# Seven products for every pair of the second feed-forward, with 56 sums made ahead

## The chip, the core and the metric

The kernel runs on one core of a Trainium2 chip. The core has a matrix engine (TensorE, PE in the profile), VectorE (DVE), ScalarE (ACT), GpSimd (POOL) and SyncE (SP), which run side by side and wait for each other through semaphores. Data lies in DRAM, in SBUF (128 partitions) and, for the results of matmuls, in 8 banks of PSUM. SP and GpSimd issue the transfers of this kernel; 16 DMA engines carry them out. The metric is the time of one execution on the device in microseconds.

## The reference

One layer of a streaming encoder, on 256 tokens of 2048 features in float32: a SwiGLU feed-forward, a block that mixes a linear recurrence and an RG-LRU branch under gates, a cross-attention to 256 memory tokens, a second SwiGLU feed-forward, and a last norm. In short:

```python
x = x + 0.5 * swiglu(rms_norm(x, ffn1_norm), ffn1_w_up, ffn1_w_down)
h = rms_norm(x, mix_norm); proj = h @ w_in
x = x + (sigmoid(gate_a) * (y_a @ w_branch_a) + sigmoid(gate_b) * (y_b @ w_branch_b)) @ w_out
x = x + cross_attention(rms_norm(x, xattn_norm), rms_norm(mem, mem_norm), wq, wkv, wo)
x = x + 0.5 * swiglu(rms_norm(x, ffn2_norm), ffn2_w_up, ffn2_w_down)
return rms_norm(x, final_norm)

def swiglu(h, w_up, w_down):
    gate, up = split(h @ w_up, 2)          # w_up: 2048 x 11264
    return (silu(gate) * up) @ w_down      # w_down: 5632 x 2048
```

All weights are float32 and are read from DRAM once; the matmuls that follow keep nearly float32 precision.

## The kernel before

**Three matmuls for one.** A float32 value is cut into a high and a low part: ACT rounds `raw` into the high part `h`, DVE subtracts to get the low part `l` (helper `split`). A product is then three fast matmuls: high by high, high by low, low by high (helper `three`). Every weight tile of 128 x 2048 (1 MiB) is loaded by SP into a buffer `raw`, split into `h` and `l`, and multiplied; the next weight tiles are asked for two ahead (`weights`, `prepare`).

**The feed-forward.** The up-projection runs over 11 groups `g` of 512 hidden features (512 gate and 512 up columns) and in each over 8 pairs `p`, each of 256 input features. A pair is a product of 2 x 2 blocks: two halves of the tokens and two blocks of 128 features on one side, those blocks and gate or up on the other. There are three ways to do it (`PRODUCTS`, `ffn_order`):

- `plain`: eight products of blocks, 24 matmuls of 512 columns, into four sums in PSUM. Buffers: `raw`, `h`, `l`.
- `fast`: seven products (a Strassen-Winograd scheme), 21 matmuls, into seven sums. It needs four sums of weight blocks (`td`) beside the weights, so a pair takes the buffers `raw`, `td`, `h`, `l` and the two parts of `td` (`h` and `tl`), six in all. On the side of the tokens it needs sums `xs` of the operand's blocks.
- `mixed`: eight products, laid so that they add into the seven sums of a group whose other pairs are fast.

When a group is done, its sums are added up (tile `ev`), go through SiLU and the product, are transposed, split (`hidop`), and wait for the down-projection, whose tiles (`wd`) are laid between the later groups.

**Sums made ahead.** A fast pair's four sums `td` cost DVE four subtractions on its way. For the pairs in the table `MADE` of the second feed-forward they are made earlier, in the middle of the program between the two feed-forwards, where DVE has time. `make_sums` lets GpSimd load the weight tile into a buffer `made`, DVE subtract in place four times, and GpSimd write the tile to DRAM (`kept`). In the second feed-forward SP then loads three quarters of the weight tile into `raw` and the finished sums into `td` (`td<-kept`). `make_ahead` spreads the makes evenly over the weight tiles of the middle.

**Buffers.** All these tiles come from one ring of nine buffers of 8 KiB a partition, `big`. While a feed-forward's own pools are open, four more belong to it; those of the second open only when the last tile of the middle's pools is done with.

**The order.** The code only records operations. A planner (`Flow.arrange`) then plays them through with a price for each (`Flow.price`), hands out buffers, and fixes the order in which each engine's instructions stand. A transfer is priced by its bytes and by a fixed time until it has landed (1.9 us before); a buffer counts as free once the planner believes that its last user is done. On the chip each engine goes through its instructions strictly in that order and waits for semaphores. Since one helper emits everything, all rows of the profile carry one line, L464, and tiles are told apart by name.

Of the kernel before, what the change touches and what calls it, by code (L numbers as in the profile page):

```python
# [14 lines left out]
P = 128  # L15
T = 256
# [4 lines left out]
NG = DFF // 512  # L21
# [9 lines left out]
for _name, _n in [  # L31
# [9 lines left out]


MIXED = {
    "ffn1": {1: (0, 2, 4, 6), 3: (6,)},
    "ffn2": {1: (4, 6), 3: ()},
}
MADE = [(g, p) for g in range(1, NG) for p in range(8) if p not in ((4, 6) if g < 3 else (1, 2, 3, 5, 6))]


def ffn_order(name):  # L50
    mixed = MIXED[name]
    out, down = [("plain", 0, p) for p in range(8)], [("down", 0, 1, c, 0) for c in range(4)]
    for g in range(1, NG):
        if g < 3:
            out += [("mixed" if p in mixed[1] else "fast", g, p) for p in (0, 1, 2, 3, 5, 4, 7, 6)]
        else:
            out += [("mixed" if p in mixed[3] else "fast", g, p) for p in (1, 3, 0, 6, 4, 2, 5, 7)]
        if g > 2 and g % 2:
            down = [("down", g - 2, 2, c, b) for c in range(4) for b in (g - 2, g - 1)]
        n = 2 if g < 3 else 4  # L60
        out, down = out + down[:n], down[n:]
    return out + [("down", NG - 2, 2, c, b) for c in range(4) for b in (NG - 2, NG - 1)]
# [116 lines left out]
LAG = {"PE": 0.24, "DVE": 0.15, "ACT": 0.16, "POOL": 0.16, "SP": 0.1}  # L179
# [4 lines left out]
class Flow:  # L184
# [69 lines left out]
    def price(self, op, method, args, kw, outs):  # L254
        q = op.queue.name
        n = outs[0].cells.size if outs else 0
        if method == "dma_start":
            n = n or args[1].cells.size
            op.moved = n * 512 / 2 ** 20 * (5.2 if "accum_op" in kw else 2.9)
            op.busy = 0.9 if q == "POOL" else 0.06  # L260
        elif method == "transpose":
            op.busy += 0.099
        elif q == "PE":
            op.busy += n / 2400 + 0.0137 if not op.turn else 0.021 if n <= 32 else 0.07 + n * 1.05e-3
        elif q == "DVE":
            n = max(n, kw["in_"].cells.size) if method == "tensor_reduce" else n
            per = {"reciprocal": 6.2, "tensor_tensor_scan": 2.2}.get(method, 1.042)
            op.busy = n * per / 1000 + 0.07
        elif q == "ACT":
            op.busy = n * 0.838e-3 + 0.095 + (0.1 if "accum_out" in kw else 0)  # L270
            op.table = args[2] if args[2] in TABLES else None
        else:
            op.busy = 1.0
# [16 lines left out]
    def arrange(self):  # L290
# [2 lines left out]
        ops = self.ops  # L293
        for op in ops:
            op.after = [a for a in getattr(op, "extra", ())]
            op.spent = op.busy + LAG[op.queue.name] + (op.moved + 1.9 if op.moved else 0)
        for op in ops:
            op.waits = len(op.deps)
            for d in op.deps:
# [20 lines left out]
        dma = reached = 0.0  # L320
# [19 lines left out]
        while events:  # L340
            t, e = heappop(events)
            if free[e] > t + 1e-9:
                continue
            while later[e] and later[e][0][0] <= reached + AHEAD:
                enter(heappop(later[e])[2])
            best, soon = None, 1e18
            for op in cand[e]:
                if best is not None and (not last or best.turn or op.due - STICK > best.due):
                    break
                if best is not None and not op.turn:  # L350
                    continue
                r = op.ready
                if op.moved:
                    r = max(r, dma - BACKLOG)
                if r <= t + 1e-9:
                    for ring in {x.ring for x in op.takes}:
                        fit = ring.fit(op, self)
                        r = max(r, fit[-1][0] if fit else 1e18)
                if r <= t + 1e-9:
                    best = op  # L360
                else:
                    soon = min(soon, r)
            if best is None:
                if soon < 1e17:
                    heappush(events, (soon, e))
                continue
            op = best
            cand[e].remove(op)
            op.start = t
            sequence.append(op)  # L370
            busy = op.busy
            if op.table is not None and op.table != table:
                table = op.table
                busy += 1.3
            if e == "PE":
                busy += 0.1 * (op.turn != last)
                last = op.turn
            free[e] = t + busy
            op.end = t + busy + LAG[e]
            if op.moved:  # L380
                dma = max(dma, t + busy) + op.moved
                op.end = dma + 1.9
            woken = {e}
            if e == "PE" and op.nominal > reached:
                reached = op.nominal
                woken.update(names)
            for ring in {x.ring for x in op.takes}:
                fit = ring.fit(op, self)
                for x in op.takes:
                    if x.ring is ring:  # L390
                        f = fit.pop(0)
                        ring.take(op, f)
                        x.place = f[1]
                        scope = ring.places[f[1]][0].scope
                        if scope is not None:
                            self.opened = max(self.opened, scope)
                            live[scope] += 1
                        if f[2] is not None:
                            for u in f[2].users:
                                if u is not op:  # L400
                                    u.extra.append(op)
                woken.update(names)
            if op.scope is not None:
                live[op.scope] -= 1
            for x in op.tiles:
                x.left -= 1
                x.ends = max(x.ends, op.end)
                if not x.left:
                    x.ring.free.append((x.ends, x.place, x))
                    if x.ring.places[x.place][0].scope is not None:  # L410
                        live[x.ring.places[x.place][0].scope] -= 1
                    woken.update(names)
            for s in op.after:
                kind = s.deps[op]
                if kind is None:
                    r = t
                elif s.queue is op.queue and not op.moved:
                    r = t + busy + (0.1 if kind and e in ("DVE", "ACT") else 0)
                else:
                    r = op.end  # L420
                s.ready = max(s.ready, r)
                s.waits -= 1
                if not s.waits:
# [45 lines left out]
def block_kernel(tc: tile.TileContext, xT, xin, memT, vec, gfin, bgate, lruw, wu1, wd1, win, wv,  # L469
                 wg, wab, wout, wq, wk, wvm, wo, wu2, wd2, out_):  # L470
    flow = Flow(tc)
    pe, dve, act, sp, gps = flow.queues
# [26 lines left out]
    def slot(dt=F32, name="slot"):  # L499
        return slots.tile([P, 1024], dt, name=name, tag="slot")  # L500
# [4 lines left out]
    def bank(name="acc"):  # L505
        return psum.tile([P, 512], F32, name=name, tag="acc")
# [17 lines left out]
    xt = [const.tile([P, 4 * T], F32, name=f"x{q}") for q in range(4)]  # L524
    x = [xt[k // 4][:, (k % 4) * T:(k % 4 + 1) * T] for k in range(KT)]
    ident = col("ident", 0, P)
# [34 lines left out]
    between = len(plan)  # L561
# [16 lines left out]
    between = between + 2, len(plan) - between - 6  # L578
# [22 lines left out]
    sums_kept, makers = {}, []  # L601

    def make_ahead(i):
        n, pieces = len(MADE), between[1]
        if 0 <= i < pieces:
            for j in range(i * n // pieces, (i + 1) * n // pieces):
                makers.append((i + 2, make_sums(*MADE[j])))
        while makers and (makers[0][0] == i or i == pieces):
            makers.pop(0)[1]()
# [222 lines left out]
        act.activation(o, acc[:, :T], ACT.Copy)  # L832
        return o

    def turned(tile, n=2):

        accs = [bank(), bank()]
        for m in range(4):
            for t in range(2):
                pe.transpose(accs[m // 2][:, m % 2 * T + t * P:][:, :P], tile[:, t * 512 + m * P:][:, :P], ident)  # L840
        return accs

    def normed(ops, c, gain):

# [564 lines left out]
    accs = []  # L1409
    for g in range(8):  # L1410
# [4 lines left out]
        if g % 2:  # L1415
            merge(g // 2, accs)
            accs = []
# [7 lines left out]
    for c in range(4):  # L1425
        accs = [bank(), bank()]
# [12 lines left out]
    for m in range(KT):  # L1439
        acc = product(xs3.tiles, weights("q", m), late)  # L1440
# [77 lines left out]

    def to_ffn(c):
        out = []  # L1520
        sums2.append(operand_pairs("ffn2", turned(xt[c]), "ffn2_norm", c, slot(name="xg"), out))
        pairs2.extend(out)
        if c < 2:
            sums2.pop(0)()

    for c in range(4):
# [129 lines left out]
```

## Time and profile before

| | us |
|---|---|
| median of 3 runs | 2453.64 (2452.77 to 2455.08) |
| the profiled execution's own time | 2456.57 |
| its span | 2454.8 |
| PE busy | 2423.6 |
| DVE busy | 2010.7 |
| ACT busy | 1405.8 |
| GpSimd busy | 61.7 |

605 MB move in the span, 247 GB/s on average. The first feed-forward runs until about 690 us, the middle until about 1760, the second feed-forward from there to the end. A row of a group gives the count, then busy time and mean duration (ns), then the idle time of the engine just before such instructions and what ended it. PE's matmuls overlap: one lasts 0.39 us in the records, and the next starts 0.23 us after it.

### The profile page before, as it was taken

How to read it: one execution, taken by the hardware profiler on the slowest of the kernel's cores; microseconds unless marked ns; L12 is line 12 of the kernel's file. 1: busy time of each engine (PE TensorE's matmuls, PEld its weight loads, DVE VectorE, ACT ScalarE, POOL GpSimd, SP SyncE). 2: the span in 40 equal slices, each digit the busy share in tenths (PEclk: the TensorE clock that was granted, in tenths of full speed). 3: DMA queues.
4: the chain of work that ended last, by engine and by line, in shares of the span. 5: the costliest groups of instructions: out<-in, count | busy, mean ns of one | idle time of the engine just before them, and what ended most of it. 6: DMA issues, size and time to landing. Idle time of an engine off the chain costs nothing. (4 is left out here: it accounts for less than half of the span.)

```text
span 2454.8 us, 30751 instructions
## 1 busy us (share of the span) xinstructions
PE 2423.6 (99%) x12166; PEld 2018.0 (82%) x12166; DVE 2010.7 (82%) x2171; ACT 1405.8 (57%) x1408; POOL 61.7 (3%) x102
## 2 busy tenths in 40 slices
PE   9999999999999999999999999999999999999998
PEld 8888888888888887888788788888878788888887
DVE  8999999999855767687676777667769999999995
ACT  8566666666654443576434644545646566666663
POOL 0000000000000000000000000000000000000000
PEclk9999999999999999999999999999999999999999
DMA  8567888778745566767777676666787666666672
GB/s 308 188 228 257 257 260 254 257 251 264 243 152 196 203 243 218 275 242 272 260 269 268 241 292 243 259 227 232 290 321 286 242 244 244 244 244 244 244 287 111
DMA packets 89712, 605.14 MB, mean 247 GB/s; under 512 B 9952, under 2 KB 10208, under 8 KB 21472
## 3 DMA queue, kind: packets, MB, share of 16 engines
q1 hardware_dynamic: 75024, 501.38, 55.5%
q0 software_dynamic: 13824, 100.67, 13.3%
q8 instruction: 95, 1.56, 0.2%
q10 hardware_dynamic: 720, 1.13, 0.1%
q14 instruction: 49, 0.40, 0.0%
HBM read 538.13 MB, written 39.85 MB: 235 GB/s over the span
## 5 line engine op out<-in xcount | busy, mean ns | idle before, releaser
L464 DVE TENSOR_TENSOR l<-raw,h 128x2048 fp32r<-128x2048 f32 (+2 forms) x428 | 875.7, 2051 | 226.3 <-ACT h L464 115.8
L464 ACT ACTIVATE h<-raw 128x2048 fp32r<-128x2048 f32 (+2 forms) x428 | 736.6, 1725 | 536.0 <-PE acc L464 145.1
L464 PE MATMUL acc<-h,xh 128*128 128x512 f32 x1248 | 469.9, 391 | 2.8 <-ACT h L464 2.4
L464 PE MATMUL acc<-h,xl 128*128 128x512 f32 x1248 | 449.9, 389 | 0.0
L464 PE MATMUL acc<-h,hidop 128*128 128x512 f32 x1408 | 442.2, 390 | 0.0
L464 PE MATMUL acc<-h,ops 128*128 128x512 f32 x1664 | 412.5, 392 | 1.2 <-DVE gate L464 1.2
L464 ACT ACTIVATE h<-td 128x1024 fp32r<-128x1024 f32 (+1 forms) x244 | 286.8, 1182 | 208.3 <-DVE td L464 182.8
L464 PE MATMUL acc<-ops,h 128*128 128x512 f32 x1152 | 392.7, 398 | 0.4 <-DVE ops L464 0.4
L464 PEld LDWEIGHTS acc<-h,ops 128*128 128x128 f32 x1664 | 311.1, 188 | 65.5 <-DVE gate L464 1.5
L464 DVE TENSOR_TENSOR tl<-td,h 128x1024 fp32r<-128x1024 f32 (+1 forms) x244 | 333.0, 1373 | 22.1 <-ACT h L464 14.4
L464 PEld LDWEIGHTS acc<-h,hidop 128*128 128x128 f32 x1408 | 262.9, 188 | 53.9 <-ACT ev L464 0.2
L464 PE MATMUL acc<-ops,l 128*128 128x256 f32 x1152 | 273.6, 282 | 8.1 <-DVE l L464 8.1
L464 PEld LDWEIGHTS acc<-h,xh 128*128 128x128 f32 x1248 | 233.5, 188 | 56.1 <-ACT h L464 7.4
L464 PEld LDWEIGHTS acc<-h,xl 128*128 128x128 f32 x1248 | 234.3, 188 | 48.6
L464 PE MATMUL acc<-l,hidop 128*128 128x512 f32 x704 | 265.8, 389 | 0.0
L464 PEld LDWEIGHTS acc<-ops,l 128*128 128x128 f32 x1152 | 213.4, 190 | 29.0 <-DVE l L464 9.0
L464 PEld LDWEIGHTS acc<-ops,h 128*128 128x128 f32 x1152 | 203.2, 189 | 32.1 <-DVE ops L464 0.7
L464 PE MATMUL acc<-l,ops 128*128 128x512 f32 x832 | 221.0, 389 | 0.0
L464 PE MATMUL acc<-l,xh 128*128 128x512 f32 x688 | 198.8, 390 | 0.0
L464 PEld LDWEIGHTS acc<-l,ops 128*128 128x128 f32 x832 | 155.6, 188 | 32.2
L464 PE MATMUL acc<-tl,xh 128*128 128x512 f32 x560 | 174.3, 391 | 0.3 <-DVE tl L464 0.2
L464 PEld LDWEIGHTS acc<-l,hidop 128*128 128x128 f32 x704 | 132.2, 188 | 27.4
(172 smaller groups left out, 1893.2 us busy)
## 6 DMA issues: line engine op xcount, KB each, us to landing
raw<-wu SPq DMA_DIRECT2D x128, 1024.0 KB, 6.8
raw<-wd SPq DMA_DIRECT2D x72, 1024.0 KB, 6.3
raw<-win SPq DMA_DIRECT2D x40, 1024.0 KB, 4.8
made<-wu POOLq DMA_DIRECT2D x36, 1024.0 KB, 5.2
kept<-made POOLq DMA_DIRECT2D x36, 1024.0 KB, 6.2
td<-kept SPq DMA_DIRECT2D x36, 1024.0 KB, 6.6
raw<-wg SPq DMA_DIRECT2D x32, 1024.0 KB, 5.4
raw<-wu SPq DMA_DIRECT2D x36, 768.0 KB, 4.3
```

Of the source, the lines that this page charges most:

```text
L464: getattr(op.queue.real, method)(*map(real, args), **{k: real(v) for k, v in kw.items()})
```

## The change

In the second feed-forward the first group and the four mixed pairs of the second and third group become fast pairs (`MIXED`), so that all 88 pairs take seven products. `MADE` grows from 36 pairs to 56: all 24 of the first three groups, and four instead of three of the eight in each later group (pair 2 is added to 0, 4 and 7). The makes are spread over 16 weight tiles fewer, so they end earlier. In the planner, transfers that GpSimd issues are reckoned to land later: 3.2 us with an accumulation, 4.6 for a load into SBUF, 5.8 for a write to DRAM, and 1.9 as before for all others. For the first group's operand sums, the third quarter's are now made before the feed-forward begins, and the last quarter of x is transposed in halves, so that one bank is taken at a time.

```diff
 MIXED = {
-    "ffn1": {1: (0, 2, 4, 6), 3: (6,)},
-    "ffn2": {1: (4, 6), 3: ()},
+    "ffn1": {0: "plain", 1: (0, 2, 4, 6), 3: (6,)},
+    "ffn2": {0: "fast", 1: (), 3: ()},
 }
-MADE = [(g, p) for g in range(1, NG) for p in range(8) if p not in ((4, 6) if g < 3 else (1, 2, 3, 5, 6))]
+MADE = [(g, p) for g in range(NG) for p in range(8) if p in ((0, 2, 4, 7) if g > 2 else range(8))]
...
-    out, down = [("plain", 0, p) for p in range(8)], [("down", 0, 1, c, 0) for c in range(4)]
+    out, down = [(mixed[0], 0, p) for p in range(8)], [("down", 0, 1, c, 0) for c in range(4)]
...
+            op.lands = 1.9 if q != "POOL" else 3.2 if "accum_op" in kw else 4.6 if op.tiles - {args[0].tile} == set() else 5.8
...
-            op.spent = op.busy + LAG[op.queue.name] + (op.moved + 1.9 if op.moved else 0)
+            op.spent = op.busy + LAG[op.queue.name] + (op.moved + op.lands if op.moved else 0)
...
-                op.end = dma + 1.9
+                op.end = dma + op.lands
...
-        n, pieces = len(MADE), between[1]
+        n, pieces = len(MADE), between[1] - 16
...
-        sums2.append(operand_pairs("ffn2", turned(xt[c]), "ffn2_norm", c, slot(name="xg"), out))
+        halves = turned(xt[c]) if c < 3 else (turned_half(xt[c], y) for y in range(2))
+        sums2.append(operand_pairs("ffn2", halves, "ffn2_norm", c, slot(name="xg"), out))
         pairs2.extend(out)
-        if c < 2:
+        if c < 3:
             sums2.pop(0)()
```

Two places where the order of instructions moves. In the rows, the numbers of the buffers are kept; they rise in the order in which the planner lays the tiles down.

The first place is on DVE in the middle of the program, while the first half's recurrence ends: the last of the four subtractions in a buffer `made`, and the split that is the next to use that buffer, which has to wait for GpSimd's write (a semaphore `DMASW`). Before:

```order
L464 TENSOR_TENSOR made_7274<-made_7274 128x512 [waits DVE_49]
L464 TENSOR_TENSOR ya_7283<-acc_7220,ostd_7332 128x256 [waits DVE_49]
L464 RECIPROCAL ostd_7332<-ostd_7332 128x256
L464 SCALAR_TENSOR_TENSOR ya_7283<-ya_7283,vt_74,silu_5987 128x256 [waits DVE_49]
L464 TENSOR_TENSOR ya_7283<-acc_7221,ostd_7332 128x256 [waits DVE_49]
L464 TENSOR_TENSOR plain_7337<-plain_7337,rstd_5469 128x256
L464 SCALAR_TENSOR_TENSOR ya_7283<-ya_7283,vt_74,silu_5987 128x256 [waits DVE_49]
L464 TENSOR_TENSOR plain_7337<-acc_7285,lo_7399 128x256 [waits Activation_49]
L464 TENSOR_TENSOR plain_7337<-plain_7337,rstd_5469 128x256 [waits DVE_49]
L464 TENSOR_TENSOR l_7414<-raw_7217,h_7270 128x2048 [waits DMAHW1_49,DMASW7_49]
```

The same stretch of the program in the changed kernel:

```order
L465 TENSOR_TENSOR made_7124<-made_7124 128x512 [waits DVE_49] x3
L465 TENSOR_TENSOR l_7221<-raw_7084,h_7139 128x2048 [waits DMAHW6_49,DMASW7_49]
L465 TENSOR_TENSOR plain_7129<-acc_7131,lo_7243 128x256 [waits PE_49,Activation_49]
L465 TENSOR_TENSOR l_7254<-raw_7181,h_7235 128x2048 [waits DMAHW7_49,PE_49]
L465 RECIPROCAL ostd_7248<-ostd_7248 128x256 [waits Activation_49]
L465 TENSOR_TENSOR plain_7129<-plain_7129,rstd_5469 128x256 [waits DVE_49]
L465 TENSOR_TENSOR ya_7289<-acc_7170,ostd_7248 128x256 [waits DVE_49]
L465 RECIPROCAL ostd_7248<-ostd_7248 128x256
L465 TENSOR_TENSOR l_7309<-raw_7191,h_7275 128x2048 [waits DMAHW0_49,DMASW3_49,Activation_49]
```

Between the last subtraction and the split that takes the buffer (l_7414 before, l_7309 now) stood eight short operations; now there are two other splits and five short operations. (The split l_7221 waits for another, earlier write.)

The second place is SP's queue at the end of the cross-attention, where the first weight tiles of the second feed-forward (`wu2`) follow the last of `wo`. Before:

```order
L464 DMA raw_13638<-wo 128x2048
L464 DMA raw_13668<-wu2 128x2048
L464 DMA raw_13745<-wu2 128x2048
L464 DMA raw_13782<-wu2 128x2048
L464 DMA raw_13815<-wu2 128x2048
L464 DMA raw_13848<-wu2 128x2048
```

In the changed kernel:

```order
L465 DMA raw_13825<-wo 128x2048
L465 DMA raw_13866<-wu2 128x1536
L465 DMA td_13870<-kept0_0_6461 128x2048
L465 DMA raw_13974<-wu2 128x1536
L465 DMA td_13976<-kept0_1_6639 128x2048
L465 DMA raw_14015<-wu2 128x1536
L465 DMA td_14020<-kept0_2_6842 128x2048
```

Each pair of the first group now takes two transfers and two buffers at this point where it took one.

More of the change, by code (lines that the diff above doesn't have):

```diff
@@ L833, in by_feature, with turned_half, turned @@
         return o
-    def turned(tile, n=2):
-        accs = [bank(), bank()]
-        for m in range(4):
+    def turned_half(tile, y):
+        acc = bank()
+        for m in (2 * y, 2 * y + 1):
             for t in range(2):
-                pe.transpose(accs[m // 2][:, m % 2 * T + t * P:][:, :P], tile[:, t * 512 + m * P:][:, :P], ident)
-        return accs
+                pe.transpose(acc[:, m % 2 * T + t * P:][:, :P], tile[:, t * 512 + m * P:][:, :P], ident)
+        return acc
+    def turned(tile):
+        return [turned_half(tile, y) for y in range(2)]
     def normed(ops, c, gain):
```

## The prediction

> **What bounds the kernel now.** I read the page's first part, then the waits of the matrix engine (PE), then windows by stage, and last the timeline around each large wait.
>
> ```profile
> span 2454.8 us, 30751 instructions
> PE 2423.6 (99%) x12166; PEld 2018.0 (82%) x12166; DVE 2010.7 (82%) x2171; ACT 1405.8 (57%) x1408; POOL 61.7 (3%) x102
> ```
>
> PE is busy for 99% of the span, so time is won in two ways only: fewer matmuls, or fewer of PE's waits. The waits, by who ended them (total, times, longest):
>
> ```profile
> PE acc L464 <- DVE l L464: 8.1, 2, 5.6
> PE acc L464 <- DVE merge L464: 3.4, 3, 1.6
> PE acc L464 <- ACT h L464: 2.4, 3, 1.3
> PE acc L464 <- DVE p L464: 2.0, 2, 1.4
> PE acc L464 <- DVE x L464: 1.2, 3, 0.6
> PE acc L464 <- DVE gate L464: 1.2, 1, 1.2
> ```
>
> The largest group is two waits for a split's low half, `l`. The timeline shows where both come from. At 928.00 GpSimd issues the write of finished sums to DRAM. VectorE (DVE) runs out of work at 931.73 and then idles 5.61 us, until that write has landed, because its next split was laid into the buffer being written out. PE waits 5.55 us for that split. At 1394.74 the same thing happens with a wait of 2.56 us.
>
> ```profile
> 926.96 0.63 DVE L464 TENSOR_TENSOR made<-made 128x512 f32<-128x512 f32 x1
> ...
> 928.00 0.54 POOL L464 DMA_DIRECT2D kept<-made  x1 [11.93 <-DVE ya L464]
> 931.31 0.42 DVE L464 TENSOR_TENSOR plain<-plain,rstd 128x256 f32<-128x256 f32 x1
> 937.35 4.49 DVE L464 TENSOR_TENSOR l<-raw,h 128x2048 fp32r<-128x2048 f32 x2 [5.61 <-DMA kept<-made]
> 939.69 0.58 PE L464 MATMUL acc<-ops,l 128*128 128x256 f32 x1 [5.55 <-DVE l L464]
> ...
> 1394.74 0.54 POOL L464 DMA_DIRECT2D kept<-made  x1 [11.80 <-DVE sum L464]
> 1401.33 2.29 DVE L464 TENSOR_TENSOR l<-raw,h 128x2048 fp32r<-128x2048 f32 x1 [1.55 <-DMA kept<-made]
> 1403.67 1.57 PE L464 MATMUL acc<-ops,l 128*128 128x256 f32 x11 [2.56 <-DVE l L464]
> ```
>
> The windows (length; busy time of PE, PEld, DVE, ACT, POOL; granted clock; DMA share; GB/s):
>
> ```profile
> 829.00:1750.00 921.00, 904.95 (x5074) 761.56 (x5073) 651.87 (x795) 462.43 (x553) 35.85 (x66) 0.99 0.69 253
> 937.90:944.70 6.80, 5.01 (x16) 4.40 (x17) 6.80 (x4) 1.91 (x1) 0.00 (x0) 0.50 0.39 154
> 1214.40:1217.80 3.40, 3.40 (x10) 2.63 (x9) 3.26 (x5) 0.57 (x2) 0.00 (x0) 0.50 0.44 130
> 1800.00:1830.00 30.00, 28.73 (x129) 23.07 (x128) 19.27 (x15) 13.45 (x11) 1.07 (x2) 1.00 0.97 367
> 1830.00:1860.00 30.00, 29.03 (x128) 24.05 (x129) 26.67 (x24) 18.82 (x14) 0.54 (x1) 1.00 0.85 337
> 2000.00:2200.00 200.00, 199.91 (x889) 163.66 (x888) 199.32 (x177) 125.31 (x99) 0.00 (x0) 1.00 0.68 250
> 2200.00:2400.00 200.00, 199.81 (x895) 164.34 (x894) 199.60 (x181) 122.68 (x99) 0.00 (x0) 1.00 0.67 250
> 20.00:40.00 20.00, 20.00 (x90) 16.58 (x89) 18.97 (x29) 19.70 (x30) 0.00 (x0) 1.00 1.01 405
> ```
>
> Three things are to be seen. After the 5.55 us wait the clock was granted at 0.50 for 6.8 us, so the wait cost more than itself (the other such stretch, at 1214.4, follows waits for `merge`). In the second feed-forward's body (2000 to 2400) PE and DVE are both full and PE waits for nothing. Its second group (1800 to 1830) is where the transfers are nearly saturated, 0.97 of the engines at 367 GB/s, and there PE loses time; these are its two waits:
>
> ```profile
> 1826.36 0.50 PE L464 MATMUL acc<-h,xh 128*128 128x512 f32 x1 [0.90 <-ACT h L464]
> 1830.97 0.50 PE L464 MATMUL acc<-h,xh 128*128 128x512 f32 x1 [1.33 <-ACT h L464]
> ```
>
> **The matmuls removed.** A pair by eight products takes 24 matmuls, by seven 21. The first group has eight such pairs and the second and third two each: 12 pairs, 36 matmuls. The step of one, from a plain pair of the second feed-forward's first group:
>
> ```profile
> 1771.28 0.39 PE L464 MATMUL acc<-h,xh 128*128 128x512 f32 x1
> 1776.72 0.39 PE L464 MATMUL acc<-h,xh 128*128 128x512 f32 x1
> ```
>
> Between these two starts lie the 24 matmuls of one pair: 5.44 / 24 = 0.2267 us each. 36 x 0.2267 = 8.2 us, all of it on the engine that has no idle time there: -8.2. That the change does this much is not in doubt; the order has 36 matmuls fewer.
>
> **The landings in the planner.** The planner reckoned a write by GpSimd to land 1.9 us after its bytes had moved; it now reckons 5.8. This moves the split that takes the freed buffer. Before, 4.1 us of DVE work stood between the last sum (ended 927.6) and that split. In the new order, at the place shown in the section on the change, stand two splits of 2.28, two reciprocals of 1.74 and three short operations of about 0.4: 9.3 us. The rows for the durations, and for the landings:
>
> ```profile
> 925.30 1.74 DVE L464 RECIPROCAL ostd<-ostd 128x256 f32<-128x256 f32 x1
> ...
> L464 DVE TENSOR_TENSOR l<-raw,h 128x2048 fp32r<-128x2048 f32 x272 | 620.6, 2287 | 222.2 <-ACT h L464 113.2 <-PE acc L464 72.3 <-DMA kept<-made 18.8
> L464 DVE TENSOR_TENSOR l<-raw,h 128x1536 fp32r<-128x1536 f32 x140 | 244.9, 1749 | 4.0 <-ACT h L464 2.6 <-PE acc L464 0.9 <-DVE tl L464 0.2
> L464 DVE TENSOR_TENSOR tl<-td,h 128x2048 fp32r<-128x2048 f32 x36 | 82.2, 2284 | 14.1 <-ACT h L464 6.6 <-PE acc L464 6.2 <-issue 1.1
> L464 DVE TENSOR_TENSOR made<-made 128x512 f32<-128x512 f32 x144 | 99.0, 687 | 35.0 <-DMA made<-wu 32.6
> ...
> made<-wu POOLq DMA_DIRECT2D x36, 1024.0 KB, 5.2
> kept<-made POOLq DMA_DIRECT2D x36, 1024.0 KB, 6.2
> td<-kept SPq DMA_DIRECT2D x36, 1024.0 KB, 6.6
> raw<-wu SPq DMA_DIRECT2D x36, 768.0 KB, 4.3
> ```
>
> A median write lands 6.2 us after its issue, and the one that hurt took 9.35; 9.3 us of other work covers both. To be won are the 8.1 us of waits and the clock's share: of the 6.8 us at 0.50, PE worked 5.01, and at full clock would have needed half, so 2.5. That makes -10.6 if every such wait goes, 0 if they come back elsewhere. The low end of the wait is nearer by the order, since nearly every taker now has 6 to 10 us of work ahead of it; but there are 56 writes instead of 36, so I leave 1.6 for stragglers: -9.0.
>
> Row first, then the rule on what such a wait costs: the waits of 0.90 and 1.33 us left the clock at 1.00, that of 5.55 did not. The Trainium skill (TensorE: Matmul & The Clock Gate, Part 1: The HAM clock gate) says that the array falls to half rate after an idle window of about 3.4 us, and recovers after one busy window. The trace agrees (0.50 for 6.8 us). By rule and row the wait carries 2.5 us beyond itself; if that clock were an accident of one run, the term would be -6.5 instead of -9.0.
>
> **Twenty more sums made ahead.** Each is a load and a write by GpSimd and four subtractions. DVE gains 80 x 0.687 = 55 us in the middle of the program, where it is busy 652 of 921 us (71%); it goes to 77%. The transfers gain 40 x 1.05 = 42 MB there, 253 + 46 = 299 GB/s; 405 has been reached. Both stay beside PE's work. What they can do is stand ahead of a DVE operation that PE waits for: `merge`, `p`, `x` and `gate` end 7.8 us of waits today. Bounds: 0, and 20/36 of 7.8 = 4.3 if today's 36 makes were the cause of all of it. I take +2, since the merges and probabilities are mostly waits on a short chain of their own. GpSimd's own queue (3% busy) delays nobody.
>
> **The start of the second feed-forward.** Its first group changes from one 1 MiB load and 3 buffers a pair to a 768 KiB load, a 1 MiB load of sums and 6 buffers. The first 16 pairs now follow each other without a down-projection or an eight-product pair between them: 16 x 1.835 = 29.4 MB, against 16 x 21 x 0.2267 = 76.2 us of PE. That wants 385 GB/s. At 405 it takes 72.5 us and costs nothing; at 367, the nearest row (same place, same kinds of transfers), 80.1 us, a wait of 3.9; at 337, the row after it, 87.2, a wait of 11. I take 3.9. The 2.2 us that PE waits there today go, because the writes of the last sums no longer run at that time (they end 16 weight tiles earlier). Net +1.7, bounds -2.2 and +8.8. DVE needs 1.75 + 2.28 = 4.03 us a pair, 64.5 in those 76.2, plus the emptying of the seven sums and the splits of the last quarter of x: close to full, as it is in the body, where PE doesn't wait for it. What is late next if the transfers keep up is DVE's emptying of the seven sums between the first two groups, for which no down-projection covers any more; a bank or two, 1 us, within the bounds.
>
> The rule that speaks against this term: the row from 20 to 40 moved 405 GB/s. The Trainium skill (DMA: Bandwidth & Descriptors, Where 436 GB/s comes from) puts the limit of one core's HBM traffic at about 358 GB/s. By that figure the 29.4 MB would need 82.1 us (an estimate), 2.0 more than I take. The trace differs from it: 405 and 367 both lie above.
>
> **Edits that cost nothing.** From the fourth group on a fourth pair has its sums ready: DVE is relieved, but PE has no wait there to lose (199.91 of 200). Chunks of x transposed in halves are the same eight transposes. The later landings reckoned for the first feed-forward's accumulating transfers move loads there; PE has no wait to lose there either, so 0, at worst +1.
>
> **The sum.** -8.2 - 9.0 + 2.0 + 1.7 = -13.5. The profiled execution took 2456.57 us (2454.8 of it the span), so 2443.1; the median of the runs is 2453.64, 2.9 lower, so 2440.
>
> **The rivals.** *The late landings come back.* More writes under a heavier load land later than 9.3 us, and other splits are caught. For it: 42 MB more. Against it: the order's cover. If the waits stay at today's 10.6 us: -8.2 + 1.7 + 2.0 = -4.5, 2449; if they grow with the number of writes (56/36), 2455. *The start is starved.* The first 16 pairs get no more than 300 GB/s: 98 us for 76.2 of work, 21.8 of waits, net +19.6; -8.2 - 9.0 + 2.0 + 19.6 = +4.4, and two waits long enough to halve the clock add 5: 2458 to 2463. It decides from about 314 GB/s with halved clock, 299 without. Against it: 337 was moved with engines only 0.85 busy. For it: 6 buffers a pair out of 13, which can leave transfers unissued. *All waits go.* -8.2 - 10.6 and no new waits: 2435, with a little more if the merges' waits fall too.
>
> **How the numbers follow.** A measurement here tells about 0.2%, 4.9 us, from no change. The forecast, including the case that all waits go, has 0.74, and all of it is faster by more. The returning landings have 0.14, within 0.2%. The starved start, with mishaps of the same kind in the middle, has 0.12, slower. The range reaches from all waits gone and the middle's shortened a little, 2431, to the returning landings, 2455; the forecast's own is 2432 to 2448.
>
> **What would show it.** PE's wait for DVE `l` falls from 8.1 to under 2, and no window of the middle but the merges' has a clock of 0.50. DVE's idle time ended by `kept<-made` falls from 18.8. PE's instructions fall by 36 and its busy time by some 8 us. Waits for ACT `h` or DVE `tl` between the first product of the second feed-forward and 80 us later grow to 3 to 5 us, with transfers at a share of 0.95 or more. Wrong would be: new waits for `l` in the middle, or a start whose transfers stay under 0.9 while PE waits (buffers, not bandwidth).

## The result and the profile after

The changed kernel takes 2434.15 us (median of 4 runs, 2432.32 to 2436.68), the kernel before 2453.72 beside it (2452.77 to 2455.08): a ratio of 0.9921, with a 95% interval of 0.9903 to 0.9938. It is faster by 19.6 us, where 13.6 was forecast. The profiled execution took 2435.0 us, 2433.2 of it the span, which is 21.6 less than the span before.

The first lines of its page, to be held against those of before:

```profile
span 2433.2 us, 30931 instructions
...
PE 2412.0 (99%) x12130; PEld 2008.5 (83%) x12130; DVE 2071.1 (85%) x2232; ACT 1417.8 (58%) x1410; POOL 83.0 (3%) x142
```

PE has its 36 instructions fewer, DVE 60 us more work, and PE's share is 99% as before. PE's waits (total, times, longest), the largest but for the one at the program's start:

```profile
PE acc L465 <- DVE tl L465: 3.2, 6, 0.9
PE acc L465 <- ACT h L465: 1.9, 3, 1.2
PE acc L465 <- ACT xg L465: 1.3, 1, 1.3
PE acc L465 <- DVE gate L465: 1.2, 1, 1.2
PE acc L465 <- ACT ev L465: 1.1, 2, 0.6
```

The waits for `l` (8.1 before) are gone, but so are those for `merge` (3.4), `p` (2.0) and `x` (1.2), which the forecast had left standing. In their place are small ones, for `tl`, `xg` and `ev` above all; the one for `gate` (1.2) stays.

Where the 21.6 us went is read from windows that cut both spans at the same work: the first matmul, the first of the middle, the first of the second feed-forward, the transposes of its third and of its last group, the end. Before (length; busy PE, PEld, DVE, ACT, POOL; granted clock, DMA share, GB/s):

```profile
1.10:692.40 691.30, 690.12 (x3098) 571.47 (x3099) 633.07 (x695) 468.98 (x442) 20.97 (x24) 1.00 0.75 250
692.40:1759.50 1067.10, 1051.05 (x6032) 886.91 (x6031) 743.16 (x902) 527.42 (x626) 37.34 (x68) 1.00 0.66 243
1759.50:1913.70 154.20, 151.43 (x676) 124.17 (x674) 123.84 (x112) 88.91 (x73) 3.21 (x6) 1.00 0.81 302
1913.70:2396.50 482.80, 481.81 (x2142) 394.94 (x2143) 481.47 (x429) 299.33 (x237) 0.00 (x0) 1.00 0.68 249
2396.50:2454.80 58.30, 49.13 (x221) 40.48 (x219) 29.02 (x34) 21.19 (x32) 0.00 (x0) 0.96 0.30 116
```

After:

```profile
1.10:695.10 694.00, 691.46 (x3099) 571.30 (x3100) 634.21 (x695) 467.35 (x442) 20.96 (x24) 1.00 0.74 247
695.10:1744.00 1048.90, 1045.69 (x6032) 884.39 (x6031) 801.89 (x991) 523.64 (x623) 61.86 (x114) 1.00 0.79 294
1744.00:1889.10 145.10, 143.82 (x643) 117.42 (x641) 134.68 (x112) 104.96 (x83) 0.00 (x0) 1.00 0.89 343
1889.10:2374.10 485.00, 481.88 (x2142) 394.95 (x2142) 473.16 (x404) 300.80 (x230) 0.00 (x0) 1.00 0.71 261
2374.10:2433.20 59.10, 49.05 (x221) 40.43 (x219) 26.95 (x32) 21.08 (x32) 0.00 (x0) 0.95 0.29 112
```

The middle is 18.2 us shorter with the same 6032 matmul rows, the start of the second feed-forward 9.1. Against that stand 2.7 us in the first feed-forward, 2.2 in the body of the second and 0.8 at the end. Neither of the two stretches at half clock in the middle is left.

At the place where the wait of 5.55 us arose, the trace after shows on DVE the four subtractions, and GpSimd's write of their buffer issued at 908.76. The split of 918.37 takes that buffer, without idle time:

```profile
905.49 2.87 DVE L465 TENSOR_TENSOR made<-made 128x512 f32<-128x512 f32 x4
908.27 2.28 DVE L465 TENSOR_TENSOR l<-raw,h 128x2048 fp32r<-128x2048 f32 x1
...
918.37 2.23 DVE L465 TENSOR_TENSOR l<-raw,h 128x2048 fp32r<-128x2048 f32 x1
```

DVE's idle time that a write of sums ended fell from 18.8 us to 5.9, and that which a load into `made` ended from 32.6 to 8.7:

```profile
DVE made L465 <- DMA made<-wu: 8.7, 7, 2.2
DVE l L465 <- DMA kept<-made: 5.9, 2, 5.4
```

### The profile page after: what moved, and what is told of

Same layout as the page of the kernel before. It is cut to its first block, busy times and chain, and to the rows that moved or that the text cites. A ratio compares the mean times of both kernels' runs of the same rounds, so it can differ in the third digit from the quotient of the medians.

```text
span 2433.2 us, 30931 instructions
## 1 busy us (share of the span) xinstructions
PE 2412.0 (99%) x12130; PEld 2008.5 (83%) x12130; DVE 2071.1 (85%) x2232; ACT 1417.8 (58%) x1410; POOL 83.0 (3%) x142
## 3 DMA queue, kind: packets, MB, share of 16 engines
q8 instruction: 95, 1.56, 0.2%
## 5 line engine op out<-in xcount | busy, mean ns | idle before, releaser
L465 ACT ACTIVATE h<-td 128x1024 fp32r<-128x1024 f32 (+1 forms) x248 | 307.8, 1249 | 171.2 <-DVE td L465 131.8
L465 DVE TENSOR_TENSOR tl<-td,h 128x1024 fp32r<-128x1024 f32 (+1 forms) x248 | 359.2, 1460 | 10.1 <-ACT h L465 7.9
L465 PE MATMUL acc<-tl,xh 128*128 128x512 f32 x608 | 189.3, 392 | 3.3 <-DVE tl L465 3.2
L465 PE MATMUL acc<-l,xh 128*128 128x512 f32 x636 | 187.6, 390 | 0.0
L465 DVE TENSOR_TENSOR made<-made 128x512 f32<-128x512 f32 x224 | 153.5, 689 | 13.0 <-DMA made<-wu 8.7
```

The costliest lines, as they stand in the source:

```text
L465: getattr(op.queue.real, method)(*map(real, args), **{k: real(v) for k, v in kw.items()})
```

## The experiments

Each ratio stands against the kernel before, run beside it on the same chip (medians there 2453.14, 2452.26, 2453.03 and 2451.35 us). Every profile is of one run. That of before took 2.9 us more than its kernel's median, so up to so much of a difference between it and another trace can belong to that run alone.

| run | edit | median, us (range) | ratio, 95% interval |
|---|---|---|---|
| e1_landings_only | before, with the new landings | 2435.36 (2435.06 to 2436.99) | 0.9929, 0.9917 to 0.994 |
| e2_old_landings | after, with the old landings | 2452.32 (2445.23 to 2471.88) | 1.001, 0.9988 to 1.0032 |
| e3_old_products | after, with the old products | 2438.79 (2436.25 to 2440.94) | 0.9943, 0.993 to 0.9956 |
| e4_old_sums | after, with the old 36 sums | 2448.60 (2447.09 to 2452.45) | 0.9983, 0.9975 to 0.9992 |
| e5_no_gap | after, makes spread to the end | 2459.87 (2456.71 to 2463.34) | 1.0027, 1.0015 to 1.0038 |
| e7_write_landing | before, the write's landing alone | 2437.47 (2436.20 to 2438.48) | 0.9938, 0.9926 to 0.995 |
| e8_write_later | e1 with 9.7 for the write | 2435.51 (2433.11 to 2437.16) | 0.9931, 0.9917 to 0.9945 |
| e11_write_3_8 | e1 with 3.8 for the write | 2437.15 (2436.31 to 2437.72) | 0.9937, 0.9924 to 0.9951 |
| e12_write_other | before, the writes hold no buffer | 2439.77 (2437.72 to 2440.63) | 0.995, 0.9936 to 0.9963 |
| e9_longer | after, with longer landings | 2435.92 (2433.06 to 2437.04) | 0.9929, 0.9916 to 0.9941 |
| e6_48_sums | after, with 48 sums | 2444.95 (2435.92 to 2447.89) | 0.9964, 0.9949 to 0.9979 |
| e10_48_longer | e6 with longer landings | 2439.66 (2437.43 to 2440.97) | 0.9946, 0.9933 to 0.9958 |

### The landings alone

```diff
+            op.lands = 1.9 if q != "POOL" else 3.2 if "accum_op" in kw else 4.6 if op.tiles - {args[0].tile} == set() else 5.8
-            op.spent = op.busy + LAG[op.queue.name] + (op.moved + 1.9 if op.moved else 0)
+            op.spent = op.busy + LAG[op.queue.name] + (op.moved + op.lands if op.moved else 0)
-                op.end = dma + 1.9
+                op.end = dma + op.lands
```

> The kernel before with one edit: the planner reckons the landings of GpSimd's transfers as the changed kernel does (3.2, 4.6, 5.8 us). Products and sums stay as before. Theory (the late writes of the sums were the waits): PE's 8.1 us of waits for DVE l and the 2.5 us of halved clock after the longer one go, so 2443 us (2441 to 2446), with under 2 us of PE waiting for l. Rival (any other laying of the order would have moved those waits, the landings have no part in it): waits of the same size turn up elsewhere, 2450 to 2456 us.

Not one matmul less, and yet 17.8 us of the 19.6, some 6 us below the theory's range. Its middle, cut as above:

```profile
693.70:1738.50 1044.80, 1044.61 (x6032) 884.11 (x6031) 744.63 (x902) 528.88 (x626) 37.15 (x68) 1.00 0.68 249
```

That is 22.3 us less than before for the same work: PE is idle for 0.2 of it. Before it was idle for 16.0, and lost another 4.2 at half clock (2.5 after the wait for `l`, and 1.7 at 1214.40, where it worked for all 3.40 us); the 2 us that are left are not assigned. All else in this run is as before to within 1.3 us a stage. The change and this run can't be told apart by their times: the interval of the change holds this run's ratio.

### The rest without the landings

```diff
-            op.lands = 1.9 if q != "POOL" else 3.2 if "accum_op" in kw else 4.6 if op.tiles - {args[0].tile} == set() else 5.8
+            op.lands = 1.9
```

> The changed kernel with all landings reckoned at 1.9 us again; seven products and 56 sums stay. Theory: waits of DVE for kept<-made come back, 8 to 16 us of them reaching PE (56 writes instead of 36), so 2442 to 2450 us. Rival: the new order is free of them by other means (fewer weight tiles for the makes, other products), 2432 to 2437 us.

The products and the sums alone win nothing that can be measured in the median, which lies 2 us above the theory's range. The trace, of a run of 2447.05 us, shows what is won and what is not. The start of the second feed-forward takes 143.1 us, 11.1 less than before:

```profile
1759.80:1902.90 143.10, 143.05 (x642) 117.80 (x642) 135.18 (x111) 104.87 (x82) 0.00 (x0) 1.00 0.90 346
```

But the middle takes 1066.6 us, as before: PE idles for 14.4 of it, with two stretches of 6.8 us at half clock. DVE's idle time ended by writes of sums is larger than before (18.8):

```profile
DVE l L465 <- DMA kept<-made: 28.5, 8, 6.7
```

So the late landings do come back with 56 makes where the order doesn't reckon with them, and not only those of the writes. PE's longest wait there, 5.09 us for an `h` at 1443.05, goes back at least in part to a load: it was issued at 1428.53 and DVE idled until it had landed, and the sum that ACT takes before that `h` stood behind.

```profile
1438.00 2.14 DVE L465 TENSOR_TENSOR made<-made 128x512 f32<-128x512 f32 x3 [3.82 <-DMA made<-wu]
```

The runs also scatter over 27 us; those of the change scatter over 4. What the slower ones lose was not traced.

### The products, the sums, and the gap after them

Three runs each undo one of the other edits. The first keeps all 56 sums but takes the old products (12 sums are then made for nothing):

```diff
-    "ffn2": {0: "fast", 1: (), 3: ()},
+    "ffn2": {0: "plain", 1: (4, 6), 3: ()},
```

> The changed kernel with the old products: the first group of the second feed-forward plain, two pairs each of the second and third mixed; the 56 sums are still made, 12 of them for nothing. 36 matmuls more. Theory (PE is full at that place and the transfers keep up): 36 x 0.2267 = 8.2 us slower than the changed kernel, 2442 to 2443 us. Rival (seven products at the start cost waits of transfers that the plain group hides): 2437 to 2440 us.

It is 4.6 us slower than the changed kernel, a time in the rival's range; the two intervals overlap. At their place the 36 matmuls are worth less than the 9.1 us above, since this run, with the old products, has a start of 150.5 us:

```profile
1740.10:1890.60 150.50, 150.50 (x676) 124.46 (x675) 117.37 (x101) 90.95 (x73) 0.00 (x0) 1.00 0.72 270
```

So 3.7 of the 9.1 come without the new products, most of them the 2.8 us that PE waited there before, and 5.4 with them: seven products save busy time, but PE waits 1.3 us that it doesn't wait with the old ones, as the rival said. The second keeps the products but makes the old 36 sums:

```diff
-MADE = [(g, p) for g in range(NG) for p in range(8) if p in ((0, 2, 4, 7) if g > 2 else range(8))]
+MADE = [(g, p) for g in range(1, NG) for p in range(8) if p not in ((4, 6) if g < 3 else (1, 2, 3, 5, 6))]
```

> The changed kernel with the old table of 36 sums: the first group's eight pairs take seven products with their sums made on the way, and so do the four pairs that were mixed and pair 2 of the later groups. Theory (VectorE is the next bound at the start): a pair costs DVE 1.22 + 2 x 0.68 for the sums beside 1.75 and 2 x 1.22 for the splits, 6.8 us against 4.8 of PE; over eight pairs some 16 us too much, less the 5 or so done ahead, so 10 to 15 us slower than the changed kernel, 2444 to 2452 us, with PE waiting for DVE in the first 50 us of the second feed-forward. Rival (the sums ahead are not needed there): within 3 us of the changed kernel, 2431 to 2437 us.

Its middle is short (1043.6 us, PE idle 0.2), but from the start of the second feed-forward, where DVE now makes the sums on the way, PE waits for DVE. These are the largest of PE's waits from 1738 to 1900 us:

```profile
PE acc L465 <- DVE tl L465: 3.8, 7, 1.0
PE acc L465 <- DVE xl L465: 3.5, 2, 2.4
PE acc L465 <- DVE l L465: 2.2, 3, 1.7
```

It loses 14.5 us to the changed kernel, as the theory had it: seven products there pay only with their sums made ahead. The third spreads the 56 makes over the whole middle:

```diff
-        n, pieces = len(MADE), between[1] - 16
+        n, pieces = len(MADE), between[1]
```

> The changed kernel with the makes spread to the end of the middle, as before, instead of ending 16 weight tiles earlier. The last six or so writes then run beside the start of the second feed-forward, where 29 MB move in 80 us at a share of 0.96. Theory (the start is close to the limit of the transfers): some 6 x 2.1 MB more at 382 GB/s, of which half fall into that stretch, 8 to 16 us of transfers against 3 us of slack, so PE waits 4 to 10 us there: 2437 to 2444 us. Rival (there is room): 2431 to 2436 us.

Neither range held: this is the starved start. The first 80 us of the second feed-forward, and a stretch within them, without the gap:

```profile
1744.00:1824.00 80.00, 64.13 (x250) 48.76 (x249) 66.77 (x69) 47.28 (x42) 4.80 (x9) 0.89 0.93 365
1776.00:1812.00 36.00, 24.18 (x87) 18.17 (x86) 26.25 (x25) 17.99 (x15) 1.06 (x2) 0.82 0.95 382
```

And in the changed kernel:

```profile
1744.00:1824.00 80.00, 78.72 (x352) 64.11 (x351) 71.95 (x59) 62.14 (x53) 0.00 (x0) 1.00 0.96 378
1750.00:1770.00 20.00, 19.09 (x86) 15.89 (x87) 19.15 (x22) 17.69 (x20) 0.00 (x0) 1.00 1.01 418
```

Without the gap GpSimd still makes sums there (nine instructions), the transfers carry 365 GB/s, not much less than 378, and PE works 64 us of 80, with the clock at 0.89. Over its first three groups it waits for 16.5 us, one wait of 6.61 for an `l`. So a low rate is not the cause. The DMA engines are nearly full (a share of 0.93 over the 80 us), part of what they carry is for the makes, and single transfers land late. The longest wait shows it:

```profile
1775.27 0.54 POOL L465 DMA_DIRECT2D made<-wu  x1
...
1787.06 1.91 ACT L465 ACTIVATE h<-td 128x2048 fp32r<-128x2048 f32 x1 [6.22 <-DMA td<-kept]
1787.53 1.42 DVE L465 TENSOR_TENSOR made<-made 128x512 f32<-128x512 f32 x2 [6.12 <-DMA made<-wu]
1788.86 1.75 DVE L465 TENSOR_TENSOR l<-raw,h 128x1536 fp32r<-128x1536 f32 x1
1790.67 0.80 PE L465 MATMUL acc<-l,xh 128*128 128x512 f32 x1 [6.61 <-DVE l L465]
```

The window of that time:

```profile
1776.00:1786.00 10.00, 7.65 (x30) 4.95 (x28) 4.40 (x3) 3.41 (x2) 0.00 (x0) 1.00 1.02 427
```

DVE idles 6.12 us until GpSimd's load into `made`, issued 12 us before, has landed; the split `l` that PE waits for stands behind its subtractions. The sums that SP loads for the next pairs land as late (ACT idles 6.22 us for them), while the share of the DMA engines is 1.02. The other waits of this stretch were not followed. The gap of 16 tiles is worth 25.7 us; without it the whole gain is lost.

### Which landing, and how long

The write's landing alone, 5.8, with loads and accumulations left at 1.9:

```diff
-            op.lands = 1.9 if q != "POOL" else 3.2 if "accum_op" in kw else 4.6 if op.tiles - {args[0].tile} == set() else 5.8
+            op.lands = 1.9 if q != "POOL" or "accum_op" in kw or op.tiles - {args[0].tile} == set() else 5.8
```

> The kernel before with one number changed: only the write of finished sums is reckoned to land 5.8 us after its bytes; GpSimd's loads and accumulating transfers stay at 1.9. The landings alone gave 2435.4 us. Theory (the late writes held up VectorE's next split and, in front of it, SP's queue of weight loads, 89.6 us of waits before): nearly all of that gain comes from this one number, 2434 to 2439 us, and SP's waits for kept<-made fall from 89.6 us to under 30. Rival (the loads of the sums, or the first feed-forward's accumulations, count as well): 2442 to 2449 us.

14.8 us of the gain come with this one number (middle 1046.6 us, PE idle 1.4), as the theory had it, though SP's waits for kept sums fell only to 36.5 us. Whether the other two landings add anything is not shown, since the intervals of this run and of e1 overlap. DVE still waits 39.1 us for GpSimd's loads into `made` there, and PE hardly notices. Longer, with all three:

```diff
-... else 4.6 if op.tiles - {args[0].tile} == set() else 5.8
+... else 4.6 if op.tiles - {args[0].tile} == set() else 9.7
```

> The kernel before with the landings of the change, but the write reckoned at 9.7 us instead of 5.8. Theory (the number has to cover what a write takes; beyond that it only holds a buffer back a little longer): 2434 to 2438 us, as with 5.8. Rival (5.8 happened to give a good laying of the order): a time anywhere between 2434 and 2454 us, most likely over 2441.

As the theory had it, no more is won. Half way:

```diff
-... else 4.6 if op.tiles - {args[0].tile} == set() else 5.8
+... else 4.6 if op.tiles - {args[0].tile} == set() else 3.8
```

> The run with the landings alone, with the write's landing at half way, 3.8 in place of 5.8. Theory (what counts is how much of a write's 6 us is reckoned with): between the two, 2437 to 2446 us, with 30 to 60 us of SP's waits for kept sums. Rival (any other laying of the rows does it): 2434 to 2437, with SP's waits under 20 us.

The time is at the lower end of the theory's range and just beyond the rival's: 3.8 gives nearly all. The planner adds this to 2.9 us for moving 1 MiB, so it reckons 6.7 us from issue to landing, where it reckoned 4.8 before, and the median write takes 6.2. The run also takes apart a reading that I held by then. A load of SP's into a buffer that a write still holds stops SP's whole queue. These waits of SP's queue were 89.6 us before:

```profile
SPq L464 <- DMA kept<-made: 89.6, 17, 9.6
```

With 3.8 they are still 53.2, and PE's idle time in the middle is 1.8 us:

```profile
SPq L465 <- DMA kept<-made: 53.2, 20, 8.2
```

So this sum is no price: such a wait can hide, presumably behind the weight tiles asked for ahead. In the trace of before, its long waits at about 850, 970, 1170 and 1500 us (8 to 10 each) have no wait of PE near them.

The changed kernel with longer landings, 7.0 for loads and 8.0 for writes:

```diff
-... else 4.6 if op.tiles - {args[0].tile} == set() else 5.8
+... else 7.0 if op.tiles - {args[0].tile} == set() else 8.0
```

> The kernel after with both of GpSimd's landings reckoned longer: 7.0 for its loads and 8.0 for its writes. Theory (the rest of the waits in the middle comes from landings that are still reckoned short: SP's queue waits 21.4 us for kept sums after the change, TensorE loses 3.2 us in the middle): SP's waits for kept sums fall under 8 us, the middle's lost 3.2 us go to under 1, and the time is 2431 us (2428 to 2434). Rival (how the rows happen to lie, not the length of the landings): SP's waits stay at 10 to 40 us and the time is anywhere from 2434 to 2440.

The theory is refuted and the rival's ranges held: the time did not fall (2435.92), PE still idles 1.8 us in the middle, and SP's waits rose. In the changed kernel, and then in this run:

```profile
SPq L465 <- DMA kept<-made: 21.4, 5, 7.4
```

```profile
SPq L465 <- DMA kept<-made: 36.6, 10, 8.3
```

From 3.8 up, a longer landing only lays the rows in another way, worth a microsecond or two in either direction.

### The writes that hold no buffer

All the runs above change the order with the landing. This one keeps every instruction of the kernel before in its place, but the writes copy their 1 MiB from DRAM, so that nothing waits for them to free a buffer. The bytes written stay the same, though a write may now start before its sums are done. The finished sums are left out: the second feed-forward loads plain weights in their place, so only its times are of use.

```diff
-                for method, args, kw in op.parts:
+                for method, args, kw, *other in op.parts:
+                    if other:
+                        args = args[0], other[0]
...
             gps.dma_start(kept, raw)
+            flow.ops[-1].parts[-1] += (wu2[g, p],)
```

> The kernel before with every instruction in its old place on every engine, but GpSimd's 36 writes copy their 1 MiB from the weights in DRAM and no longer from the buffer made, so that nobody waits for a write to give a buffer free (the sums kept are left out: the second feed-forward then works with wrong ones). Theory (the middle's lost time comes of buffers that a late write holds, whatever the order): TensorE's waits for l and for merge go, no halved clock in the middle, SP's 89.6 us of waits for kept go, and the time is 2435 to 2439 us, as with the new landings. Rival (the new order did it, by other things than the freed buffers): waits of 10 us or more stay in the middle and the time is 2448 to 2454.

2439.77 us, 11.6 less than the kernel before beside it, 0.8 above the theory's range. The middle:

```profile
692.70:1745.40 1052.70, 1046.99 (x6033) 883.78 (x6032) 741.88 (x900) 525.74 (x626) 36.65 (x68) 1.00 0.65 246
```

PE's waits:

```profile
PE acc L466 <- DVE merge L466: 2.4, 3, 1.5
PE acc L466 <- ACT h L466: 1.3, 4, 0.6
PE acc L466 <- DVE x L466: 1.2, 2, 0.9
PE acc L466 <- DVE l L466: 1.1, 2, 0.8
```

The wait for `l` falls from 8.1 to 1.1 and no stretch at half clock is left: in the old order, the held buffers cost 14.4 of the 22.3 us. GpSimd's loads gain little by it: they end 30.6 us of DVE's idle time, against 32.6 before. The waits for `merge` stay (2.4 of 3.4), so these are not the buffers' but the order's. The other 8 us of e1 come from rows laid differently, and which rows do it was not isolated.

### Fewer sums for the later groups

The body's 2.2 us came with the fourth sum made ahead. With three (48 in all):

```diff
-MADE = [(g, p) for g in range(NG) for p in range(8) if p in ((0, 2, 4, 7) if g > 2 else range(8))]
+MADE = [(g, p) for g in range(NG) for p in range(8) if p in ((0, 4, 7) if g > 2 else range(8))]
```

> The changed kernel with 48 sums: all 24 of the first three groups, three instead of four in each later group. Theory (the seven products at the start gave their 8 to 9 us, but the 20 more sums took back 4.1 us in the middle and 2.3 us in the body): the body's 2.3 us go and 8/20 of the 4.1, so 2430 us (2428 to 2432). Rival (the fourth pair's sums relieve VectorE in the body): slower than the changed kernel, 2436 to 2440 us.

It missed both ranges, at 2444.95. The traced run is the slowest of nine (2447.89); three of the nine took 2436 to 2437 us. The body behaves as expected; from 1959 to 2387 PE waits for nothing although DVE is full:

```profile
1959.00:2387.00 428.00, 427.99 (x1907) 351.26 (x1906) 426.89 (x383) 264.75 (x209) 0.00 (x0) 1.00 0.67 250
```

The changed kernel in its body, 431 us with DVE less busy, and PE's waits from 1943 to 2376:

```profile
1943.00:2374.00 431.00, 428.30 (x1907) 352.02 (x1906) 419.23 (x359) 266.18 (x204) 0.00 (x0) 1.00 0.70 259
```

```profile
PE acc L465 <- DVE tl L465: 1.6, 3, 0.6
PE acc L465 <- ACT ev L465: 1.1, 2, 0.6
```

But the middle was long in this run (1057.9 us, PE idle 8.7: `merge` 3.3, `x` 3.7, `h` 1.7), although it has fewer makes, and the first groups lose time too: the second feed-forward takes 684.6 us from its first matmul to the last, against 679.2 in the changed kernel. With the longer landings of e9 as well:

> The kernel with 48 sums, now with the same longer landings. Theory (its 45.4 us of SP's waits and its lost 8.7 us in the middle came of landings reckoned too short): SP's waits fall under 10 us, the groups of the second feed-forward stay at 61.1 us, and the time is 2430 us (2428 to 2433). Rival (48 sums lie badly in the middle by themselves): 2436 to 2448, with the waits of the run before still there.

The time lies between that run and the changed kernel, in the rival's range, and the theory's 2430 is refuted; SP's waits for kept sums are 35.2 us, not under 10. The middle recovers (1049.9 us, PE idle 3.7), the body keeps its groups of 61.1 us, yet the second feed-forward takes 683.7 us from its first matmul to the last, against 679.2 in the changed kernel: the first groups lose more than the body wins. Where the pairs with all sums ready end, DVE has no free moment, PE waits 1.63 us after eight transposes (`acc<-vt,ev`), and the clock falls:

```profile
1919.29 1.26 PE L465 MATMUL acc<-vt,ev 128*128 128x128 f32 x8 [0.24 <-ACT ev L465]
1922.18 1.21 PE L465 MATMUL acc<-h,xh 128*128 128x512 f32 x2 [1.63 <-ACT h L465]
```

The window around it (clock 0.83):

```profile
1920.00:1930.00 10.00, 8.37 (x31) 6.50 (x32) 10.00 (x10) 8.48 (x8) 0.00 (x0) 0.83 0.24 80
```

No version that was run beats the changed kernel.

## Why the prediction was right, and where its sizes were off

The sign, the range and the kinds of term held; the sizes did not, and two errors partly cancel. By the prediction's steps, against the trace:

- **The matmuls, -8.2.** They went, but were worth less. The first three groups are 9.1 us shorter than before, yet e3, with the old products, has 3.7 of these 9.1 too. The new products take 6.7 us off PE's busy time there and bring 1.3 of waiting: 5.4 at their place, and 4.6 in the whole.
- **The landings, -9.0.** The mechanism was right, the size wrong by more than half: -22.3 in the trace of the run with the landings alone, -17.8 in its time (the traced run of before was 2.9 us above its median). The step that failed is "To be won are the 8.1 us of waits and the clock's share": it counted only PE's waits whose releaser was named `l`. With the landings alone the 16.0 us of waits in the middle went but for 0.2, and both stretches at half clock. The same step's lower bound, "-10.6 if every such wait goes", fell with it. Shown is that held buffers make 14.4 of it in the unchanged order (11.6 of the 17.8 in the times); the other 8 come with the new order, by rows that were not isolated. That `merge` and `p` would go with a new order couldn't be read from their releasers, and I had set them aside as "waits on a short chain of their own". The step also reckoned with writes alone: loads into `made` land late too, and held up PE in e2 (9.5 us after the issue) and in e5 (12.2).
- **Twenty more sums, +2.** At the upper bound: 1048.9 against 1044.8 us, +4.1, of which 3.0 is idle time (3.2 against 0.2). That the sums are the cause is not shown: the lay of the rows alone moves the middle as much, and e8, with 36 sums, takes 1048.0. In the body, where they were priced at nothing, 2.2 came with a fourth made pair: DVE is relieved as foretold, 419 of 431 us, and PE waits all the same, for `tl` and `ev`. What is late there, the loads or the buffers, stays open.
- **The start, +1.7.** It took -0.9 beside 8.2 for the matmuls. That the old waits there go was right (none in e3); the new products wait 1.3 us, for `xg`, in place of 3.9. The transfers carried 378 GB/s over 80 us, between the 367 that I took and the 405 that I didn't. The Trainium skill (DMA: Bandwidth & Descriptors, Where 436 GB/s comes from) has some 358 GB/s as the limit of a core's HBM traffic; this trace moved 378 over 80 us and 418 over 20, so the measurement decides against it here.
- **The first feed-forward, 0 to +1.** It took 2.7 more, but the other runs with its landings lie between 691.1 (e3) and 693.5 us (e5), so no cause is assigned. The end took 0.8 more, which was not followed up.

The sum, with the start's 9.1 us split as forecast: -8.2 - 0.9 - 22.3 + 4.1 + 2.7 + 2.2 + 0.8 = -21.6, where the prediction had -13.5.

Of the rivals, *all waits go* gave 2435 and came nearest, with the right mechanism and too small a price for it. That it came so near is luck: it had 10.6 for the landings' 22.3, and nothing for the 9.8 us that were lost elsewhere (4.1 + 2.7 + 2.2 + 0.8). *The late landings come back* is what happens without the new landings (e2: 2452). *The starved start* is what happens without the gap (e5: 2460, in the range foretold for it), but not by its condition: I set it at 299 to 314 GB/s, and e5 starved at 365, with loads and makes sharing full engines. Of what was to show it, the fall of the waits for `l`, the clock in the middle, the 36 instructions and a share of 0.95 at the start came true. The waits of 3 to 5 us there did not.

## What to carry to other kernels

Where an order is fixed ahead by a model of times, one wrong time moves every wait of the stage: price its correction by all the waits and clock losses there, not by the rows that name the late transfer, and measure it alone before it is mixed with other edits. Reckon with the landing of a transfer as the trace shows it for its queue and kind; here the step from 1.9 to 3.8 us gave nearly all. An edit that saves matmuls is worth what is left after its operands have been made elsewhere: here 5 us at the place, and in the whole 2 (against e1) to 5 (against e3), which the intervals don't tell from nothing.

## What was not expected of the hardware

- A few short waits can halve the clock when transposes lie between them. In e10 PE waited 0.24 and 1.63 us around 1.26 us of transposes, 3.1 us together, and lost its clock; in the kernel before, waits of 1.56 and 1.59 us around one transpose, with seven more behind them, did so. In e12 one wait of 1.48 us between one and seven transposes (2.7 us together) left the clock at 1.00. The Trainium skill (TensorE: Matmul & The Clock Gate, Part 4: PE-mode transpose) says that a transpose doesn't count as busy in the same way; the two places that lost it agree.
- A write of 1 MiB by GpSimd landed after 6.2 us in the median before and 6.4 after, and the one that hurt took 9.35; the planner's 1.9 had made 4.8 of it.
- Two of the new orders scatter far more from run to run than the others: 27 us (e2) and 12 (e6), against 1 to 7. The kernel before scatters as much as e6 (12.6 us over 23 runs). Why wasn't found out.
